# Last weight parts loaded into two gating tiles, a weight split ordered behind a copy, and four squares spread out, in a hybrid decoder layer on one core

## The chip, the cores and the metric

The kernel runs on one core of one Trainium2 chip. The metric is the time on the device of one execution, in microseconds (us). Five engines matter here: TensorE (PE in the profile) multiplies matrices, VectorE (DVE) and ScalarE (ACT) do elementwise work, GpSimd (POOL) and SyncE (SP) mostly issue DMA transfers. Each engine takes its own instructions strictly in order. An instruction that has to wait holds up everything behind it on that engine, and a DMA issue that has to wait holds up all later DMA issues of the same engine.

## The reference, cut to what matters

The reference is one decoder layer for 512 tokens of width 1024 in float32: a gated feed-forward block (22 blocks of 128 hidden columns on each side), a mixer of a state-space scan and differential attention, cross-attention into a memory, a second feed-forward block, and a last norm. The change touches the two feed-forward blocks.

```
def rms_norm(x, w):
    y = x32 * lax.rsqrt(jnp.mean(x32 * x32, axis=-1, keepdims=True) + EPS)
    return y.astype(x.dtype) * w

def swiglu(h, w_in, w_out):
    gate, up = jnp.split(h @ w_in, 2, axis=-1)
    return (jax.nn.silu(gate) * up) @ w_out

x = x + 0.5 * swiglu(rms_norm(x, norm_ffn1_w[l]), ffn1_w_in[l], ffn1_w_out[l])
x = x + hybrid_mixer(...)
x = x + memory_cross_attention(...)
x = x + 0.5 * swiglu(rms_norm(x, norm_ffn2_w[l]), ffn2_w_in[l], ffn2_w_out[l])
return rms_norm(x, norm_final_w)
```

## The kernel before, in words

Every operand of a matmul is split into a high and a low half: ScalarE copies it to a rounded high half (`wh` for a weight, `s31h`, `g11h` and so on for activations), VectorE subtracts to get the low half (`wl`, `s31l`, `g11l`), and TensorE adds three products, high by high, high by low and low by high. All of that goes through the helper `split_into` (lines 155 and 156). Raw weights arrive by DMA in tiles named `wr`, of which there are six. There are three tiles each for `wh` and `wl`. A tile name with a fixed number of buffers is reused in turn, and whoever writes it next has to wait until the last reader of its earlier content is done.

The two matrix products of a feed-forward block are done in a scheme of seven products on two-by-two blocks instead of eight, with sums of weight blocks and of activation blocks as operands.

*The input side.* `quad` makes one group of four column blocks. It accumulates in three PSUM banks `qa`, `qe`, `qb` and runs seven products in this order: "11", S1, S2, "12", S3, S4, "22". Each has its own weight, split from a `wr` tile: the first to the seventh split. Between them the banks are copied: `qb<-qa` before S2 adds to `qb` (lines 284 and 289), `u<-qb` before S3 adds to `qb` (line 299), `p<-qe`. `m3` is the sixth weight, and `t4` the seventh.

*The gating.* `ffn_quads` then multiplies the banks by the norm's row, applies silu in a tile `gate`, multiplies by the other half into a tile `th`, and `block_tiles` makes the blocks and sums of `th` (`g11`, `s31`, `s24`, `g`) that are operands of the output side. `gate` and `th` (made by `s4`, four KB a partition) have one buffer each.

*The output side.* The 22 blocks are taken in three runs of 6, 8 and 8, which the code calls thirds. After the groups of a third, `out_blocks` multiplies with the output weights in banks `oa`, `oe`, `ob`, again in seven products, each in two parts of the contraction (`parts`). The first part of a product uses the early groups, and the last part uses the last groups. In the first feed-forward block the weight sums are made here: `fetch` (line 1277) issues the load of a block on SP's queue, and `added` (line 1316) adds a second block to the same tile with an accumulating DMA from POOL's queue, issued after the load has landed. `t1` is such a sum. It is the weight of the product S1 in the bank `oe`, and its raw tile stays in use to the end of `out_blocks`, since `t2` and the last product add to it. `b21` loads the weight of the product "12". In the second feed-forward block all sums are made beforehand in DRAM, and `out_blocks` there only loads.

The two products that come first, "11" in `oa` and S1 in `oe`, alternate by part: `oa` first part, `oe` first part, `oa` last part, `oe` last part. Then come S2, "12", S3, S4 and "22".

*What sets the order.* SP's and POOL's instructions stand in the order in which the code emits them. For TensorE, VectorE and ScalarE a scheduler orders the instructions by its own estimate of when each can run. The code can put an instruction behind others on the scheduler's list with `behind`.

*The last turn.* Before the second feed-forward block the residual is transposed back to tokens by rows: `turn` transposes on TensorE into `pxf` and copies into `x` on ScalarE. With `summed=True` it also squares each copied tile with a row sum (`squared`, line 551, into a tile `junk`). `row_from` turns the row sums into the norm's row, which the first gating of the second block needs.

Of the kernel before, what the change touches and what calls it, by code (L numbers as in the profile page):

```python
# [11 lines left out]
F32 = mybir.dt.float32  # L12
R32 = mybir.dt.float32r
AF = mybir.ActivationFunctionType
# [3 lines left out]
P = 128  # L18
T = 512
# [81 lines left out]
def body(tc, a, dbg=None):  # L101
# [13 lines left out]
    def nm(s):  # L115
        uid[0] += 1
        return f"{s}_{uid[0]}"
# [6 lines left out]
    def s4(s):  # L124
        return sp.tile([P, 4, T // 2], F32, tag=s, name=nm(s), bufs=1)
# [57 lines left out]
    @contextmanager  # L183
    def behind(ins):
        with ExitStack() as after:
            for i in ins:
                after.enter_context(tc.issue_after(i))
            yield

    H = T // 2  # L190
    S1, S2, S3, S4 = "S1", "S2", "S3", "S4"

    def halves(t):
        return t.rearrange("p (f t) -> p f t", f=2)

# [33 lines left out]
    def add_product(ps, w, xs, which, first, ks=None):  # L229

        wh, wl = w
        n = len(xs)
        for f in range(2):
            out = ps[:, f * H : (f + 1) * H]
            for kp in ks or range(n):
                wc = slice((f * n + kp) * P, (f * n + kp + 1) * P)
                xh, xl = xs[kp][which]
                for j, (a_, b_) in enumerate(((wh, xh), (wh, xl), (wl, xh))):
                    od.t += (H + 32) / 2400
                    newest_mm[:] = [nc.tensor.matmul(out, a_[:, wc], b_, start=first and f == 0 and kp == 0 and j == 0, stop=kp == n - 1 and j == 2, skip_group_check=True).ins]  # L240
                yield
# [9 lines left out]
    def split_w(raw):  # L251
        hi = wp.tile([P, D], R32, tag="wh", name=nm("wh"))
        lo = wp.tile([P, D], R32, tag="wl", name=nm("wl"))
        newest[:] = [split_into(hi, lo, raw)[0].ins]
        return hi, lo

    def quad(xs, src, ready, fresh=False):

        b12, b11, b22, b21 = src[0], src[1], src[2], src[3]
        m1 = raw_w(b11)
        if ready:
            t, t2, m2, m7, m3 = raw_w(ready[0]), raw_w(ready[1]), raw_w(b21), raw_w(b12, b22), raw_w(b22)
            t4 = m2
        else:
            t, m3, m2, m7 = raw_w(b12, b11), raw_w(b22), raw_w(b21), raw_w(b12, b22)  # L270
            t2 = t4 = t
        a_ps = acc("qa")
        e_ps = acc("qe")
        b_ps = acc("qb")
        w1, w5 = split_w(m1), split_w(t)
        second = list(newest)
        if fresh:

            n = len(xs)
            yield from add_product(a_ps, w1, xs, "11", True, range(n - 1))  # L280
            yield from add_product(e_ps, w5, xs, S1, True, range(n - 1))
            yield from add_product(a_ps, w1, xs, "11", False, range(n - 1, n))
            with behind(second):
                S.activation(b_ps, a_ps, AF.Copy)  # L284
            yield from add_product(e_ps, w5, xs, S1, False, range(n - 1, n))
        else:
            yield from add_product(a_ps, w1, xs, "11", True)
            with behind(second):
                S.activation(b_ps, a_ps, AF.Copy)
            yield from add_product(e_ps, w5, xs, S1, True)  # L290
        p5 = s2("p5")
        S.activation(p5, e_ps, AF.Copy)
        if not ready:
            V.tensor_tensor(t2, t, m3, ALU.add)
        yield from add_product(b_ps, split_w(t2), xs, S2, False)
        if not ready:
            V.tensor_tensor(t4, t2, m2, ALU.add)
        u2 = s2("u2")
        S.activation(u2, b_ps, AF.Copy)  # L299
        V.tensor_tensor(e_ps, e_ps, u2, ALU.subtract)  # L300
        yield from add_product(a_ps, split_w(m2), xs, "12", False)
        w7 = split_w(m7)
        if ready:
            V.tensor_tensor(t4, t2, m2, ALU.add)
        yield from add_product(b_ps, w7, xs, S3, False)
        c22 = s2("c22")
        V.tensor_tensor(c22, p5, b_ps, ALU.subtract)
        yield from add_product(e_ps, split_w(m3), xs, S4, False)
        yield from add_product(b_ps, split_w(t4), xs, "22", False)
        yield (a_ps, b_ps), (e_ps, c22)  # L310

# [238 lines left out]
    def squared(k, src):  # L550
        S.activation(s2("junk"), src, AF.Square, accum_out=squares[:, k : k + 1])

    def row_from(st, apart, rows=1.2):
        both = small("nboth", 4, bufs=2)
        V.tensor_tensor(both, squares[:, :4], squares[:, 4:], ALU.add)
        yield from st.from_sums(both, apart, rows)
# [81 lines left out]

    def bc_c(t):
        return t[:, None, :].to_broadcast([P, 4, 16])  # L640

    def flat(t):
        return t.rearrange("p a b -> p (a b)")

    def col64(s):
        return cp.tile([P, 4, 16], F32, name=s)
# [622 lines left out]
    def out_blocks(blocks, sums, g, col4, ncol4, each=None, finale=None, clean=True, n=None, by_dma=False):  # L1269
# [2 lines left out]
        n = n or len(g)  # L1272
        parts = [(k, min(k + 2, n)) for k in range(0, n, 2)]

        def fetch(of, part):
            raw = wp.tile([P, (part[1] - part[0]) * T], F32, tag="wr", name=nm("wr"), bufs=6)
            nc.sync.dma_start(raw, of[:, part[0] * T : part[1] * T])
            return raw

# [19 lines left out]
        def product(ps, of, which, first=False, ready=None):  # L1299
            for part in parts:  # L1300
                w = ready if ready and part == parts[0] else weights(of, part)
                for t in range(2):
                    yield from some(ps[t], w, which, part, t, first)
# [6 lines left out]

        t_raw = {}

        def added(of, more):
            def make(part):
                raw = fetch(of, part)
                G.dma_start(raw, more[:, part[0] * T : part[1] * T], accum_op=ALU.add)
                return raw
            return make

        def t1(part):  # L1320
            t_raw[part] = added(blocks[B12], blocks[B11])(part)
            return t_raw[part]

        def t2(part):
# [2 lines left out]
            return t_raw[part]  # L1327

        def b21(part):
            later[part] = fetch(blocks[B21], part)  # L1330
            return later[part]

        def t4(part):
            G.dma_start(t_raw[part], blocks[B21][:, part[0] * T : part[1] * T], accum_op=ALU.add)
# [29 lines left out]
        for t in range(2):  # L1364
            u2.append(s2("u2"))
            S.activation(u2[t], b_ps[t], AF.Copy)
            V.tensor_tensor(e_ps[t], e_ps[t], u2[t], ALU.subtract)
        yield from product(a_ps, b21 if here and not by_dma else blocks[B21], "12")
        for part in later:
            V.tensor_tensor(t_raw[part], t_raw[part], later[part], ALU.add)  # L1370
        later.clear()
# [83 lines left out]
            yield from out_blocks(a[f"f2b{c}"], wsum[c], g, col4, ncol4, *((norm, store) if at_end else (None, None)), clean=c == 0)  # L1455

    def turn_last():
        yield from turn(1, summed=True)
        od.spawn(row_from(st_2, 8.0), 3.0)

    od.add(turn_last())
    od.add(ffn2())
# [89 lines left out]
```

## Time and profile before

| | |
|---|---|
| median of three runs | 1316.02 us (1313.1 to 1317.21) |
| the profiled execution's own time | 1314.69 us |
| its span, first to last instruction | 1312.8 us |
| TensorE busy | 1290.0 us |
| VectorE busy | 969.8 us |
| ScalarE busy | 707.5 us |
| mean granted TensorE clock | 0.998 |

The profile is of one execution. In a row of the timeline the first number is the start in us from the span's beginning, the second the length, then engine, source line, operation, output<-inputs, shape, how many were merged, and, in brackets, how long the engine had been idle before it and what ended that. SPq is SP's queue of DMA issues. A matmul's length covers the whole pipeline, and matmuls overlap, so the pace is the distance from start to start: about 0.12 us for 256 columns and 0.23 us for 512. Busy shares are averages over stages; what an edit is worth is read at its place.

### The profile page before, as it was taken

The page shows a single profiled execution, that of the slowest core. Times are in us where ns is not written, and L with a number is a line of the kernel's source. Part 1 is how long each engine was busy: PE and PEld are TensorE (multiplying, and loading weights), DVE is VectorE, ACT ScalarE, POOL GpSimd, SP SyncE. Part 2 cuts the span into 40 slices and gives each one's busy share as a digit, 9 for nine tenths or more (in the row PEclk, how much of TensorE's full clock was granted, in tenths as well). Part 3 has the DMA queues.
Part 4 walks back from the last instruction along what each step waited for, and adds up shares of the span by engine and source line. Part 5 has one row for each costly group of instructions (what it writes and reads, how often), then busy time and mean ns, then how long its engine had stood idle before and what let it go on. Part 6 is the DMA issues. An engine that isn't in the chain of part 4 may idle for free.

```text
span 1312.8 us, 20085 instructions
## 1 busy us (share of the span) xinstructions
PE 1290.0 (98%) x7710; PEld 1125.3 (86%) x7710; DVE 969.8 (74%) x1539; ACT 707.5 (54%) x1207; POOL 130.9 (10%) x153
## 2 busy tenths in 40 slices
PE   9999999999999999999999999999999999999997
PEld 7889988998887778777788878888889999989995
DVE  5987888788776676557867686745668878876886
ACT  6544554565754465346645465534365646555564
POOL 0201001001110011110103022020001000000000
PEclk9999999999999999999999999999999999999999
DMA  9357778766994434763365648684139876655652
GB/s 338 85 160 194 200 178 221 220 180 178 327 295 152 130 73 111 257 188 106 85 182 176 183 133 240 189 221 133 65 98 272 207 233 178 187 197 178 196 191 95
DMA packets 70415, 237.38 MB, mean 181 GB/s; under 512 B 8288, under 2 KB 9792, under 8 KB 69968
## 3 DMA queue, kind: packets, MB, share of 16 engines
q1 hardware_dynamic: 54208, 183.13, 40.4%
q0 software_dynamic: 13168, 45.67, 19.4%
q10 hardware_dynamic: 2944, 7.30, 1.6%
q8 instruction: 60, 0.98, 0.3%
q14 instruction: 35, 0.29, 0.1%
HBM read 233.92 MB, written 50.91 MB: 217 GB/s over the span
## 4 chain that ended last, share of the span: by engine, by line
PE 58%; issue 10%; DVE 4%; ACT 2%; DMA 1%; POOL 1%; POOLq 0%; ACTq 0%; DVEq 0%
PE pm L146 10%; PE qb L240 8%; PE qe L240 5%; PE qa L240 5%; PE pxbc L146 4%; PE ob L1296 3%; PE pcq L146 3%; PE pz L146 3%; PE oa L1296 2%; PE oe L1296 2%; PE pcv L146 2%; PE pq L146 2%; PE pv L146 1%; DVE wl L156 1%; PE pk L146 1%
## 5 line engine op out<-in xcount | busy, mean ns | idle before, releaser
L155 ACT ACTIVATE wh<-wr 128x1024 fp32r<-128x1024 f32 (+1 forms) x329 | 334.2, 1019 | 357.8 <-issue 71.2
L156 DVE TENSOR_TENSOR wl<-wr,wh 128x1024 fp32r<-128x1024 f32 (+1 forms) x329 | 384.7, 1173 | 145.7 <-ACT wh L155 141.9
L777 ACT ACTIVATE ec<-ec,mn 128x512 f32<-128x512 f32 (+3 forms) x64 | 35.3, 554 | 33.7 <-DVE mn L776 33.7
L146 PE MATMUL pxbc<-hnh,wh 128*128 128x512 f32 x128 | 52.6, 411 | 0.0
L146 PE MATMUL pxbc<-hnh,wl 128*128 128x512 f32 x128 | 50.2, 392 | 0.0
L146 PE MATMUL pxbc<-hnl,wh 128*128 128x512 f32 x128 | 50.2, 392 | 0.0
L240 PE MATMUL qb<-s31h,wh 128*128 128x256 f32 x152 | 43.2, 284 | 3.2 <-ACT u L299 3.2
L240 PE MATMUL qb<-s24h,wh 128*128 128x256 f32 x152 | 43.1, 284 | 1.3 <-ACT qb L284 1.3
L240 PE MATMUL qb<-s24h,wl 128*128 128x256 f32 x152 | 43.1, 284 | 0.5 <-DVE wl L156 0.5
L240 PE MATMUL qa<-h11h,wh 128*128 128x256 f32 x152 | 43.1, 283 | 0.0
L240 PE MATMUL qb<-s31h,wl 128*128 128x256 f32 x152 | 43.0, 283 | 0.0
L240 PE MATMUL qa<-h11h,wl 128*128 128x256 f32 x152 | 43.0, 283 | 0.0
L240 PE MATMUL qa<-hmh,wh 128*128 128x256 f32 x152 | 43.0, 283 | 0.0
L240 PE MATMUL qa<-hml,wh 128*128 128x256 f32 x152 | 43.0, 283 | 0.0
L240 PE MATMUL qe<-s24h,wh 128*128 128x256 f32 x152 | 43.0, 283 | 0.0
L240 PE MATMUL qe<-s24l,wh 128*128 128x256 f32 x152 | 43.0, 283 | 0.0
L240 PE MATMUL qe<-s24h,wl 128*128 128x256 f32 x152 | 43.0, 283 | 0.0
L240 PE MATMUL qb<-hmh,wh 128*128 128x256 f32 x152 | 43.0, 283 | 0.0
L240 PE MATMUL qb<-hml,wh 128*128 128x256 f32 x152 | 43.0, 283 | 0.0
L240 PE MATMUL qb<-hmh,wl 128*128 128x256 f32 x152 | 43.0, 283 | 0.0
L240 PE MATMUL qa<-h11l,wh 128*128 128x256 f32 x152 | 43.0, 283 | 0.0
L240 PE MATMUL qa<-hmh,wl 128*128 128x256 f32 x152 | 43.0, 283 | 0.0
(452 smaller groups left out, 4166.7 us busy)
## 6 DMA issues: line engine op xcount, KB each, us to landing
wr<-in_f2q SPq DMA_DIRECT2D x44, 512.0 KB, 4.3
wr<-in_f1q SPq DMA_DIRECT2D x40, 512.0 KB, 4.6
wr<-in_f1b SPq DMA_DIRECT2D x30, 512.0 KB, 5.4
isum<-in_f2q SPq DMA_DIRECT2D x22, 512.0 KB, 5.6
wr<-isum SPq DMA_DIRECT2D x22, 512.0 KB, 4.3
wsum<-in_f2b SPq DMA_DIRECT2D x20, 512.0 KB, 6.6
wr<-wsum SPq DMA_DIRECT2D x20, 512.0 KB, 4.6
wr<-in_f1q POOLq DMA_DIRECT2D x16, 512.0 KB, 6.5
```

What stands on the lines that cost most here:

```text
L146: newest_mm[:] = [nc.tensor.matmul(out, w, x, start=start, stop=stop).ins]
L155: S.activation(hi, src, AF.Copy),
L156: V.tensor_tensor(lo, src, hi.bitcast(F32), ALU.subtract),
L240: newest_mm[:] = [nc.tensor.matmul(out, a_[:, wc], b_, start=first and f == 0 and kp == 0 and j == 0, stop=kp == n - 1 and j == 2, skip_gr ...
L777: S.activation(ec[:, :n], ec[:, :n], AF.Exp, bias=mn, scale=-1.0, accum_out=sm[c][:, i : i + 1])
L1296: newest_mm[:] = [nc.tensor.matmul(ps, a_[:, ts], b_[:, ws], start=first and k == 0 and j == 0, stop=k == n - 1 and j == 2, skip_group_che ...
```

## The change

There are three edits.

1. In `out_blocks` of the first feed-forward block, the last part of `t1` is loaded into the tile `gate` and the last part of `b21` into the tile `th`, instead of two `wr` tiles. The loads keep their place in SP's order. `b21` is now also used by the third third.
2. In `quad`, the split of the sixth weight (`m3`) is ordered behind the copy `u<-qb`.
3. The four squares of the last turn are no longer emitted with the copies but by a new chain, one every 2.0 of the order's own time units, each behind the newest weight split. The norm's row is made after them.

```
@@ quad
-        S.activation(u2, b_ps, AF.Copy)
+        copy = S.activation(u2, b_ps, AF.Copy)
...
-        yield from add_product(e_ps, split_w(m3), xs, S4, False)
+        with behind([copy.ins]):
+            w3 = split_w(m3)
+        yield from add_product(e_ps, w3, xs, S4, False)
@@ out_blocks
-        def fetch(of, part):
-            raw = wp.tile([P, (part[1] - part[0]) * T], F32, tag="wr", name=nm("wr"), bufs=6)
+        def fetch(of, part, spare=None):
+            n = (part[1] - part[0]) * T
+            if spare and part == parts[-1]:
+                raw = flat(s4(spare))[:, :n]
+            else:
+                raw = wp.tile([P, n], F32, tag="wr", name=nm("wr"), bufs=6)
             nc.sync.dma_start(raw, of[:, part[0] * T : part[1] * T])
...
-        def added(of, more):
+        def added(of, more, spare=None):
             def make(part):
-                raw = fetch(of, part)
+                raw = fetch(of, part, spare)
                 G.dma_start(raw, more[:, part[0] * T : part[1] * T], accum_op=ALU.add)
...
-            t_raw[part] = added(blocks[B12], blocks[B11])(part)
+            t_raw[part] = added(blocks[B12], blocks[B11], "gate")(part)
...
         def b21(part):
-            later[part] = fetch(blocks[B21], part)
-            return later[part]
+            raw = fetch(blocks[B21], part, "th")
+            if not by_dma:
+                later[part] = raw
+            return raw
...
-        yield from product(a_ps, b21 if here and not by_dma else blocks[B21], "12")
+        yield from product(a_ps, b21 if here else blocks[B21], "12")
@@ turn_last
-        yield from turn(1, summed=True)
-        od.spawn(row_from(st_2, 8.0), 3.0)
+        yield from turn(1)
+        od.spawn(row_of_last(), 4.0)
+
+    def row_of_last():
+        for k in range(4, KT):
+            with behind(list(newest)):
+                squared(k, x[k])
+            yield 2.0
+        yield from row_from(st_2, 3.0)
```

What this moves is shown at three places. The first is SP's queue at the output side of the second third. The rows in turn load, before: the last part of "11", the last part of `t1` (`wr_2158`), two parts of B22, two parts of B21 (`wr_2225`, `wr_2243`) and the first part of S3's weight. In brackets stand the semaphores that a row waits for.

```order
L1277 DMA wr_2140<-in_f1b 128x1024 [waits DMAHW2_49,DMAHW6_49,DVE_49,Activation_49]
L1277 DMA wr_2158<-in_f1b 128x1024 [waits DMASW3_49,DVE_49]
L1277 DMA wr_2181<-in_f1b 128x1024 [waits DMAHW1_49,DMAHW0_49,DVE_49]
L1277 DMA wr_2200<-in_f1b 128x1024 [waits DVE_49]
L1277 DMA wr_2225<-in_f1b 128x1024 [waits DMAHW4_49,DVE_49]
L1277 DMA wr_2243<-in_f1b 128x1024 [waits DMAHW3_49,DMAHW0_49,DVE_49]
L1277 DMA wr_2265<-in_f1b 128x1024 [waits DMAHW6_49,DVE_49]
```

The same rows with the change:

```order
L1283 DMA wr_2140<-in_f1b 128x1024 [waits DMAHW2_49,DMAHW6_49,DVE_49,Activation_49]
L1283 DMA gate_2158<-in_f1b 128x1024 [waits DVE_49,Activation_49]
L1283 DMA wr_2181<-in_f1b 128x1024 [waits DMAHW0_49,DMASW3_49]
L1283 DMA wr_2200<-in_f1b 128x1024 [waits DMAHW1_49]
L1283 DMA wr_2225<-in_f1b 128x1024
L1283 DMA th_2243<-in_f1b 128x1024 [waits DMAHW3_49,DVE_49]
L1283 DMA wr_2265<-in_f1b 128x1024 [waits DMAHW4_49]
```

The load into `gate` now waits for VectorE and ScalarE, the last users of that tile: the last multiplication `th<-c,gate` and the silu of the third's last group. The load into `th` waits for VectorE, whose last use of the tile is `gl<-th,gh`. The loads between and behind them no longer wait for VectorE to free a `wr` tile.

On TensorE, at the end of the last part of "11" (`oa`) at the same place, before:

```order
L1296 MATMUL oa_2110<-wl_2143,g11h_2088 128x512
L1296 MATMUL oe_2111<-wh_2161,s31h_1920 128x512
L1296 MATMUL oe_2111<-wh_2161,s31l_1921 128x512
L1296 MATMUL oe_2111<-wl_2162,s31h_1920 128x512
L1296 MATMUL oe_2111<-wh_2161,s31h_2097 128x512
L1296 MATMUL oe_2112<-wh_2161,s31h_1920 128x512
```

With the change:

```order
L1302 MATMUL oa_2110<-wl_2143,g11h_2088 128x512
L1357 MATMUL ob_3416<-ones_r 128x512
L1302 MATMUL oe_2111<-wh_2161,s31h_1920 128x512
L1302 MATMUL oe_2111<-wh_2161,s31l_1921 128x512
L1302 MATMUL oe_2112<-wh_2161,s31h_1920 128x512
L1302 MATMUL oe_2112<-wh_2161,s31l_1921 128x512
L1302 MATMUL ob_2113<-wh_2184,s24h_1461 128x512
L1302 MATMUL ob_2113<-wh_2184,s24l_1462 128x512
L1302 MATMUL oe_2111<-wl_2162,s31h_1920 128x512
```

`wh_2161` is the high half of the weight that is now loaded into `gate`. One clearing matmul moved ahead of its first use, and two matmuls of S2 (`ob_2113`) moved in between its uses.

The second place is ScalarE in the second group of the last third, from the split of the fifth weight (`wh_2770`). `wh_2804` is the sixth weight, `wh_2832` the seventh. Before:

```order
L155 ACTIVATE wh_2770<-wr_2620 128x1024
L292 ACTIVATE p_489_2687<-qe_2624 128x512
L155 ACTIVATE wh_2804<-wr_2616 128x1024
L155 ACTIVATE s31h_2712<-s_492_2707 128x512
L155 ACTIVATE wh_2832<-wr_2613 128x1024
L299 ACTIVATE u_496_2735<-qb_2625 128x512
L155 ACTIVATE s24h_2751<-s_493_2708 128x512
L155 ACTIVATE gh_2786<-th_2605 128x512
```

With the change:

```order
L155 ACTIVATE wh_2770<-wr_2620 128x1024
L295 ACTIVATE p_489_2687<-qe_2624 128x512
L155 ACTIVATE s31h_2712<-s_492_2707 128x512
L302 ACTIVATE u_496_2735<-qb_2625 128x512
L155 ACTIVATE s24h_2751<-s_493_2708 128x512
L155 ACTIVATE wh_2804<-wr_2616 128x1024
L155 ACTIVATE gh_2786<-th_2605 128x512
L155 ACTIVATE wh_2832<-wr_2613 128x1024
```

The copy `u<-qb` moved ahead of both weight splits.

The third place is ScalarE at the start of the second feed-forward block, from the last sum of activations. `junk` is a square, `wh_9944` (with the change `wh_9936`) the fourth weight of the first group, `qb<-qa` the bank's copy that S2 waits for. Before:

```order
L155 ACTIVATE s24h_9795<-s_2040_9786 128x512
L551 ACTIVATE junk_9820,squares_232<-x_119 128x512
L551 ACTIVATE junk_9823,squares_232<-x_121 128x512
L551 ACTIVATE junk_9826,squares_232<-x_123 128x512
L551 ACTIVATE junk_9829,squares_232<-x_125 128x512
L284 ACTIVATE qb_9846<-qa_9844 128x512
L292 ACTIVATE p_2069_9910<-qe_9845 128x512
L155 ACTIVATE wh_9944<-wr_9837 128x1024
```

With the change:

```order
L155 ACTIVATE s24h_9795<-s_2040_9786 128x512
L556 ACTIVATE junk_9883,squares_232<-x_119 128x512
L155 ACTIVATE wh_9936<-wr_9829 128x1024
L287 ACTIVATE qb_9838<-qa_9836 128x512
L295 ACTIVATE p_2063_9898<-qe_9837 128x512
L556 ACTIVATE junk_9910,squares_232<-x_121 128x512
L556 ACTIVATE junk_9931,squares_232<-x_123 128x512
```

Three of the four squares moved behind the copy, and the split of the fourth weight moved ahead of it.

More of the change, by code (lines that the diff above doesn't have):

```diff
@@ L191, in body, with flat @@
     S1, S2, S3, S4 = "S1", "S2", "S3", "S4"
+    def flat(t):
+        return t.rearrange("p a b -> p (a b)")
     def halves(t):
@@ L640, in bc_c @@
         return t[:, None, :].to_broadcast([P, 4, 16])
-    def flat(t):
-        return t.rearrange("p a b -> p (a b)")
     def col64(s):
```

## The prediction

> **What bounds the kernel now.** I read the page first, then the list of waits of TensorE, then the timeline at the places that the change touches.
>
> ```profile
> span 1312.8 us, 20085 instructions
> PE 1290.0 (98%) x7710; PEld 1125.3 (86%) x7710; DVE 969.8 (74%) x1539; ACT 707.5 (54%) x1207; POOL 130.9 (10%) x153
> PE qb L240 <- ACT u L299: 3.2, 2, 1.6
> PE qb L240 <- ACT qb L284: 1.3, 1, 1.3
> PE oa L1296 <- DVE g11l L156: 0.8, 1, 0.8
> PE oe L1296 <- DVE s31l L156: 0.7, 1, 0.7
> PE qb L240 <- DVE wl L156: 0.5, 1, 0.5
> ...
> PE pt L150 <- DVE on L846: 0.2, 1, 0.2
> ```
>
> TensorE is busy for 98% of the span, and the list of its waits has only fifteen rows, the longest 3.2 us in total. So an edit can win little: what it removes is a row of this list. It can lose much more, since any new wait of TensorE goes straight into the time. The five rows shown at the top are those that the change can reach: 3.2 for the sixth weight's edit, 1.3 for the squares, and 2.0 in or just behind the output sides.
>
> **Edit 1, the loads in the gating's tiles: second third.** The weight of S1's last part is a sum of two blocks: a load from SP's queue, then an accumulating load from POOL's queue, then the split on ScalarE. Before, these stood at
>
> ```profile
> 173.75 0.33 SPq L1277 DMA_DIRECT2D wr<-in_f1b  x1
> 179.58 0.87 POOL L1316 DMA_DIRECT2D wr<-in_f1b  x1 [8.51 <-DVE wl L156]
> 187.97 0.68 DVE L450 TENSOR_TENSOR th<-c,gate 128x512 f32<-128x512 f32 x1
> 189.83 1.06 ACT L155 ACTIVATE wh<-wr 128x1024 fp32r<-128x1024 f32 x1 [2.51 <-DMA wr<-in_f1b]
> 194.49 0.39 PE L1296 MATMUL oe<-wh,s31h 128*128 128x512 f32 x1
> 198.18 0.39 PE L1296 MATMUL ob<-wh,s24h 128*128 128x512 f32 x1
> ```
>
> The load was issued at 173.75, the accumulation at 179.58, its landing let ScalarE go at 189.83, and TensorE took the result at 194.49. With the change the load goes into `gate`, and the order shows that it waits for the last reader of that tile, the multiplication that ends at 187.97 + 0.68 = 188.65. That is 14.9 us later than the issue before. Nothing on TensorE can cover this: behind the last part of `oa` the order has S1's last part, with two matmuls of S2 among the first six. And everything behind it on SP's queue waits too.
>
> For the two DMAs I have their landing times over the program (the loads of line 1277, then the accumulations of line 1316):
>
> ```profile
> DMA to landing us min/median/max: 2.6/4.6/11.6
> DMA to landing us min/median/max: 4.3/5.9/10.1
> ```
>
> From the load's issue to POOL's issue I take 4.5 us: near the median, since SP's queue will be empty, bounded by the least landing, 2.6, and by the 179.58 - 173.75 = 5.8 at this place before. For the accumulation I take 6.3, a little over the median, because three held-up loads start with it; its bounds are 4.3 and the 189.83 - 179.58 = 10.2 seen here. With 1.1 for the split TensorE can start at 188.65 + 4.5 + 6.3 + 1.1 = 200.6 (196.7 to 205.8). Twelve matmuls of 512 columns at 0.227 us make 2.7, so the part ends at 203.3, where before it ended at 198.18: a loss of 5.1 us (1.2 to 10.3). This already counts the two waits of 0.8 and 0.7 on `g11l` and `s31l`, which fall into it and vanish. The load into `th` waits for the end of that group's splits, some 5 us on. Its weight is taken a whole product later, and S3's sums, queued behind it, two products later, so the same delay of TensorE covers both; I cost them at nothing here.
>
> **Last third.** The same place there:
>
> ```profile
> 310.71 2.35 DVE L156 TENSOR_TENSOR wl<-wr,wh 128x1024 fp32r<-128x1024 f32 x2
> 313.58 0.68 DVE L450 TENSOR_TENSOR th<-c,gate 128x512 f32<-128x512 f32 x1
> 318.09 0.39 PE L1296 MATMUL oe<-wh,s31h 128*128 128x512 f32 x1
> 322.02 0.39 PE L1296 MATMUL ob<-wh,s24h 128*128 128x512 f32 x1
> ```
>
> In the new order one of the two splits at 310.71 stands behind the multiplication, so `gate` is free about 1.2 us earlier than 314.26, at 313.1. The same three terms give 313.1 + 11.9 = 325.0 (321.1 to 330.2), and with the 2.7 of the twelve matmuls the part ends at 327.7 against 322.02: a loss of 5.7 us (1.8 to 10.9).
>
> **First third.** No group with `gate` comes before it, so that load is free. The load into `th` is not:
>
> ```profile
> 72.85 0.33 SPq L1277 DMA_DIRECT2D wr<-in_f1b  x1
> 76.10 0.33 SPq L1277 DMA_DIRECT2D wr<-in_f1b  x1
> 79.92 0.68 DVE L156 TENSOR_TENSOR gl<-th,gh 128x512 fp32r<-128x512 f32 x1
> 80.10 0.90 POOL L1316 DMA_DIRECT2D wr<-in_f1b  x1 [17.38 <-DVE wr L1326]
> 87.11 1.06 ACT L155 ACTIVATE wh<-wr 128x1024 fp32r<-128x1024 f32 x1
> 91.47 0.39 PE L1296 MATMUL ob<-wl,s31h 128*128 128x512 f32 x1
> ```
>
> It moves from 72.85 to the end of `gl<-th,gh`, 80.6. Behind it on SP is the load of S3's first part, at 76.10 before and about 81.0 now. With 4.0 to POOL's issue, 6.3 for the accumulation, and 1.1 and 1.2 for the high and the low half, the low half is there at 93.6, and S3's third matmul took it at 91.47: a loss of 2.1 us (none to 3.4).
>
> **The clock.** TensorE would idle for about 7 us in the second third (oa's last part ends near 193.5) and some 6 in the last. The end of the program shows what such a pause does, and its start what it costs (columns of the windows: the stretch, busy time of PE, PEld, DVE, ACT, POOL, then the granted clock):
>
> ```profile
> 1303.60:1308.10 4.50, 0.00 (x0) 0.00 (x0) 2.50 (x6) 2.18 (x5) 1.22 (x2) 1.00 0.71 265
> 1308.20:1312.80 4.60, 0.00 (x0) 0.00 (x0) 0.00 (x0) 0.00 (x0) 0.00 (x0) 0.50 0.26 98
> 6.86 0.63 PE L146 MATMUL pa<-hml,wah 128*128 128x512 f32 x1
> 7.29 0.65 PE L146 MATMUL pa<-hmh,wal 128*128 128x512 f32 x1
> ```
>
> 4.5 us after the last matmul the granted clock falls to 0.50. At the start a matmul of 512 columns takes 0.43 us instead of 0.23. I take eleven matmuls at the slow pace behind each pause, 11 x 0.2 = 2.2 us each, 4.4 in all; the bounds are nothing and twice that. The Trainium skill (TensorE: Matmul & The Clock Gate, What's actually happening) says that the array drops to half its clock after at least one idle window of about 3.4 us and needs about 3.4 us of sustained work to come back. The end of this trace agrees that it drops, after 4.5 us. By the page's window the slow stretch would cost half of 3.4 us, 1.7 a pause and 3.4 in all, an estimate from that page; the sum would be 1.0 less.
>
> **Edit 2, the sixth weight.**
>
> ```profile
> 257.41 1.06 ACT L155 ACTIVATE wh<-wr 128x1024 fp32r<-128x1024 f32 x1 [1.31 <-PE qa L240]
> 258.38 0.58 ACT L299 ACTIVATE u<-qb 128x512 f32<-128x512 f32 x1
> 259.01 0.39 PE L240 MATMUL qb<-s31h,wh 128*128 128x256 f32 x1 [1.58 <-ACT u L299]
> 301.16 0.39 PE L240 MATMUL qb<-s31h,wh 128*128 128x256 f32 x1 [1.58 <-ACT u L299]
> ```
>
> In two of the nineteen groups the seventh weight's split, which has to wait for the product "12" to give up its tile, stood ahead of the copy `u<-qb`, and S3 waited 1.58 us. In the new order the copy stands ahead of both splits in every group. The gain is 3.2 us. The sixth weight is late next: its low half now stands on VectorE behind a gating multiplication and the subtraction from `qe`, and I take 0.2 off: 3.0 (2.5 to 3.2). In the other seventeen groups the copy was in time, and nothing is won.
>
> **Edit 3, the squares.**
>
> ```profile
> 979.67 0.28 PE L240 MATMUL qe<-s31h,wh 128*128 128x256 f32 x1
> 980.63 0.61 ACT L551 ACTIVATE junk<-x 128x512 f32<-128x512 f32 x1
> 981.24 0.57 ACT L284 ACTIVATE qb<-qa 128x512 f32<-128x512 f32 x1
> 981.87 0.38 PE L240 MATMUL qb<-s24h,wh 128*128 128x256 f32 x1 [1.32 <-ACT qb L284]
> ```
>
> Three squares leave from ahead of the copy, but a weight split of 1.06 us takes their place, and it needs the tile that `qa`'s last product gives up at about 979.7. So the copy starts near 980.8 instead of 981.24: a gain of 0.5 us (0 to 1.3), not the whole wait. The row is made later, and the first gating waits for the end of the group anyway; nothing is lost there.
>
> **The sum.** Also the freed tiles let the first group after the first third load earlier; of its 0.5 us wait I take 0.3. Losses 5.1 + 5.7 + 2.1 + 4.4 = 17.3, gains 3.0 + 0.5 + 0.3 = 3.8, together +13.5 us. The profiled execution took 1314.69 us, so 1328.2. The median shown is 1.3 above that execution, well inside the spread of 4 between the three runs, so I leave the forecast at 1328.2. About 0.3%, 4 us, is what a measurement of this kernel can tell from no change.
>
> **The rivals.** *The clock holds.* A few matmuls fall into the pauses (the table's two small ones in the last third), and the pauses are near the limit seen at the end. Then the 4.4 goes: 1323.8. Against it stands that both pauses are longer than 4.5. *The two DMAs are quick.* With SP's queue empty both could take their least, 2.6 and 4.3. Then the losses are 1.2, 1.8 and 0, the pauses are too short for the clock, and with the gains the sum is -0.8: 1313.9, no change. It decides where the accumulation lands less than 8 us after the multiplication. At this very place it took 10.2 by itself before, so I give it little. *The load is not held up*, that is, the wait for `gate` is for an earlier group's use and the load still starts near 173.75. Then edit 1 costs nothing, takes away the 1.5 us on `g11l` and `s31l`, and the result is 1314.7 - 3.8 - 1.5 = 1309.4, faster. The order's row speaks against it, as it names VectorE and ScalarE and no earlier DMA. *Both accumulations are slow*, 10.2 each as seen here: 5.2 more in the second and 5.2 more in the last third, 1338.6.
>
> **Chances.** 1328 (half), clock holds 0.25, slow accumulations 0.12, quick DMAs 0.08, load not held up 0.05. The first three are slower by over 0.3%, the fourth is within it, the last is faster: 0.05, 0.08, 0.87. The range goes from 1317, between quick and middling DMAs, to 1338.
>
> **What would show it.** Right: on TensorE one wait of 5 to 9 us on the split or the DMA of `gate` in each of the second and the last third, one of 1 to 3 us at S3 in the first, granted clock under 1.00 behind the long ones, no row for `u` at S3, and a wait of about 0.8 for `qb<-qa`. It would be wrong if the load into `gate` is issued before the last group's multiplication, or if TensorE finds S2's matmuls to do meanwhile.

## The result and the profile after

The changed kernel took 1336.61 us (median of 5 runs, 1335.52 to 1338.96), the kernel before 1313.42 on the same chip (1312.38 to 1317.21). The ratio is 1.0173, with a 95% interval of 1.0159 to 1.0186: 1.7% slower. The forecast was 1328.2, with a range from 1317 to 1338.

The page and the list of TensorE's waits of the changed kernel, the rows that answer to those shown of before:

```profile
span 1334.8 us, 20083 instructions
PE 1294.1 (97%) x7710; PEld 1128.9 (85%) x7710; DVE 971.3 (73%) x1539; ACT 707.1 (53%) x1207; POOL 126.2 (9%) x153
```

```profile
PE oe L1302 <- ACT wh L155: 19.5, 2, 10.5
PE ob L1302 <- ACT wh L155: 4.3, 2, 3.6
...
PE qb L243 <- ACT qb L287: 0.8, 1, 0.8
```

Two new rows carry the loss: TensorE waits 10.5 and 9.0 us for the split of S1's last part (`oe`), and 3.6 us at S3 in the first third (`ob`). The row for `u` (3.2) is gone, `qb<-qa` went from 1.3 to 0.8.

The timeline at the second third, where the load into `gate` stands:

```profile
191.94 0.68 DVE L455 TENSOR_TENSOR th<-c,gate 128x512 f32<-128x512 f32 x1
...
192.70 0.33 SPq L1283 DMA_DIRECT2D gate<-in_f1b  x1
...
197.58 0.87 POOL L1322 DMA_DIRECT2D gate<-in_f1b  x1 [24.73 <-DMA gate<-in_f1b]
...
206.97 1.06 ACT L155 ACTIVATE wh<-gate 128x1024 fp32r<-128x1024 f32 x1 [8.98 <-DMA gate<-in_f1b]
...
208.08 0.79 PE L1302 MATMUL oe<-wh,s31h 128*128 128x512 f32 x1 [10.47 <-ACT wh L155]
```

The multiplication frees `gate` at 192.62, and the load starts 0.1 us later: it was held up by exactly that. From there it takes 5.0 us to POOL's issue, 9.4 to the split's start and 1.1 to TensorE: 15.5 in all. In the last third the same chain takes 15.0, of which the accumulation 8.9:

```profile
323.45 0.68 DVE L455 TENSOR_TENSOR th<-c,gate 128x512 f32<-128x512 f32 x1
...
324.20 0.33 SPq L1283 DMA_DIRECT2D gate<-in_f1b  x1
...
329.17 0.86 POOL L1322 DMA_DIRECT2D gate<-in_f1b  x1 [20.27 <-ACT gh L155]
...
338.06 1.06 ACT L155 ACTIVATE wh<-gate 128x1024 fp32r<-128x1024 f32 x1 [7.26 <-DMA gate<-in_f1b]
...
339.17 0.79 PE L1302 MATMUL oe<-wh,s31h 128*128 128x512 f32 x1 [9.04 <-ACT wh L155]
```

In the first third it is the load into `th` that is late, and behind it on SP the loads of S3's sums. The accumulation of S3's first part, issued at 83.43, lets the split go at 91.87, 8.4 us later, and S3 starts behind a wait of 3.6:

```profile
78.82 0.33 SPq L1283 DMA_DIRECT2D th<-in_f1b  x1
...
83.43 1.90 POOL L1322 DMA_DIRECT2D wr<-in_f1b  x2 [32.38 <-DMA wr<-in_f1b]
...
91.87 1.06 ACT L155 ACTIVATE wh<-wr 128x1024 fp32r<-128x1024 f32 x1 [5.95 <-DMA wr<-in_f1b]
...
92.98 0.79 PE L1302 MATMUL ob<-wh,s31h 128*128 128x512 f32 x1 [3.61 <-ACT wh L155]
...
100.01 0.39 PE L1302 MATMUL oe<-wh,s24h 128*128 128x512 f32 x1
```

How the DMA engines and the clock went in the second third, in stretches of 4 us (the last three columns are the granted clock, the DMA engines' busy share, which can come out a little above 1, and GB/s), after and then before:

```profile
186.00:190.00 4.00, 4.00 (x32) 3.83 (x31) 1.92 (x2) 1.95 (x2) 0.00 (x0) 1.00 0.01 4
190.00:194.00 4.00, 4.00 (x19) 3.34 (x18) 3.76 (x6) 1.94 (x4) 0.00 (x0) 1.00 0.06 16
194.00:198.00 4.00, 3.61 (x16) 2.63 (x15) 2.35 (x5) 2.55 (x5) 0.42 (x1) 1.00 0.91 248
198.00:202.00 4.00, 0.00 (x0) 0.00 (x0) 1.23 (x1) 0.00 (x0) 0.44 (x1) 0.87 1.01 396
202.00:206.00 4.00, 0.00 (x0) 0.00 (x0) 0.00 (x0) 0.00 (x0) 0.00 (x0) 0.50 1.05 286
```

```profile
186.00:190.00 4.00, 4.00 (x19) 3.32 (x18) 2.65 (x4) 1.23 (x2) 0.00 (x0) 1.00 0.92 321
190.00:194.00 4.00, 3.11 (x13) 2.05 (x12) 3.07 (x4) 3.02 (x5) 0.66 (x1) 1.00 0.23 89
```

With the change the DMA engines stand idle (share 0.01 and 0.06) while SP waits for `gate`, and are full (0.91 to 1.05) as soon as it is free: every load behind that one goes out at once, and the accumulation into `gate` has to share with them.

Where the 22 us lie is read from the starts of the same matmuls, the first of each output side and the first of the groups behind it. Before, and then after:

```profile
74.68 0.40 PE L1296 MATMUL oa<-wh,g11h 128*128 128x512 f32 x1
...
103.26 0.28 PE L240 MATMUL qa<-h11h,wh 128*128 128x256 f32 x1
...
184.85 0.40 PE L1296 MATMUL oa<-wh,g11h 128*128 128x512 f32 x1
...
225.38 0.28 PE L240 MATMUL qa<-h11h,wh 128*128 128x256 f32 x1
...
309.90 0.40 PE L1296 MATMUL oa<-wh,g11h 128*128 128x512 f32 x1
...
344.63 0.39 PE L1296 MATMUL ob<-wh,gh 128*128 128x512 f32 x1
```

```profile
72.87 0.40 PE L1302 MATMUL oa<-wh,g11h 128*128 128x512 f32 x1
...
108.17 0.28 PE L243 MATMUL qa<-h11h,wh 128*128 128x256 f32 x1
...
189.03 0.40 PE L1302 MATMUL oa<-wh,g11h 128*128 128x512 f32 x1
...
239.57 0.28 PE L243 MATMUL qa<-h11h,wh 128*128 128x256 f32 x1
...
320.83 0.40 PE L1302 MATMUL oa<-wh,g11h 128*128 128x512 f32 x1
...
367.54 0.39 PE L1302 MATMUL ob<-wh,gh 128*128 128x512 f32 x1
```

| stretch | before | after | difference | forecast |
|---|---|---|---|---|
| start to the first output side | 74.7 | 72.9 | -1.8 | 0 |
| first output side | 28.6 | 35.3 | +6.7 | +2.1 |
| groups to the second | 81.6 | 80.9 | -0.7 | -0.3 |
| second output side | 40.5 | 50.5 | +10.0 | +7.3 |
| groups to the last (edit 2) | 84.5 | 81.3 | -3.3 | -3.0 |
| last output side, to its last product | 34.7 | 46.7 | +12.0 | +7.9 |
| the rest (edit 3) | 968.2 | 967.3 | -0.9 | -0.5 |
| sum | 1312.8 | 1334.8 | +22.0 | +13.5 |

(The clock's 4.4 of the forecast stands half with the second, half with the last output side.) The -1.8 at the start is not the change's: kernels that are alike up to there start the first output side at 72.9 or at 74.6 (the changed kernel at 72.87, the one with its two long pauses filled, below, at 74.58).

### The profile page after: what moved, and what is told of

Same layout as the page of the kernel before. It is cut to its first block, busy times and chain, and to the rows that moved or that the text cites. A ratio compares the mean times of both kernels' runs of the same rounds, so it can differ in the third digit from the quotient of the medians.

```text
span 1334.8 us, 20083 instructions
## 1 busy us (share of the span) xinstructions
PE 1294.1 (97%) x7710; PEld 1128.9 (85%) x7710; DVE 971.3 (73%) x1539; ACT 707.1 (53%) x1207; POOL 126.2 (9%) x153
## 4 chain that ended last, share of the span: by engine, by line
PE 77%; issue 13%; DVE 3%; DMA 3%; ACT 2%; POOL 1%; POOLq 0%; SPq 0%; ACTq 0%; DVEq 0%
PE qb L243 12%; PE pm L146 10%; PE qa L243 8%; PE qe L243 8%; PE ob L1302 5%; PE pxbc L146 4%; PE oe L1302 4%; PE pcq L146 3%; PE oa L1302 3%; PE pz L146 3%; DMA gate<-in_f1b 2%; PE pcv L146 2%; PE pg L146 2%; PE pu L146 2%; PE pa L146 2%
## 5 line engine op out<-in xcount | busy, mean ns | idle before, releaser
L155 ACT ACTIVATE wh<-wr 128x1024 fp32r<-128x1024 f32 (+1 forms) x317 | 323.2, 1022 | 332.4 <-issue 58.8
L156 DVE TENSOR_TENSOR wl<-wr,wh 128x1024 fp32r<-128x1024 f32 (+1 forms) x317 | 372.3, 1178 | 140.0 <-ACT wh L155 138.4
L779 ACT ACTIVATE ec<-ec,mn 128x512 f32<-128x512 f32 (+3 forms) x64 | 35.3, 554 | 33.7 <-DVE mn L778 33.7
L243 PE MATMUL qb<-s31l,wh 128*128 128x256 f32 x152 | 43.1, 284 | 0.0
L243 PE MATMUL qe<-s31h,wl 128*128 128x256 f32 x152 | 43.1, 283 | 0.0
```

Of the source, the lines that this page charges most:

```text
L155: S.activation(hi, src, AF.Copy),
L156: V.tensor_tensor(lo, src, hi.bitcast(F32), ALU.subtract),
L779: S.activation(ec[:, :n], ec[:, :n], AF.Exp, bias=mn, scale=-1.0, accum_out=sm[c][:, i : i + 1])
```

## The experiments

Times are compared with runs of the kernel before on the same chip, by the ratio; a run's difference to another run is the difference of their ratios times 1314. Rows and waits of a run are from one profiled execution of it.

**Edits 2 and 3 alone.** Edit 1 is taken back:

```diff
-            t_raw[part] = added(blocks[B12], blocks[B11], "gate")(part)
+            t_raw[part] = added(blocks[B12], blocks[B11])(part)
...
-            raw = fetch(blocks[B21], part, "th")
-            if not by_dma:
-                later[part] = raw
-            return raw
+            later[part] = fetch(blocks[B21], part)
+            return later[part]
...
-        yield from product(a_ps, b21 if here else blocks[B21], "12")
+        yield from product(a_ps, b21 if here and not by_dma else blocks[B21], "12")
```

> Edit 1 is undone, the sixth weight's order and the spaced squares stay. By the prediction's own terms (3.0 for the sixth weight, 0.5 for the squares) 3.5 us under the kernel before: 1310. If these two edits carry part of the loss that the forecast missed, the time is above that of the kernel before by up to 8. If what they remove comes back as another wait, there is no difference. In the list of waits the row for u (3.2) should be gone and the one for qb behind the copy of qa should read 0.8.

Measured: 1319.46 us, ratio 1.0037 (1.0026 to 1.0049). Slower than before, though the wait on `u` was gone and that on `qb<-qa` down to 0.8, and though at the start of the last output side TensorE was 5.1 us ahead of the kernel before (304.85 against 309.90), 1.7 of them from the start of the program. On that output side it lost 9.0 us, to its last product (43.75 against 34.73), and 8.1 of them at one place, S3, with a wait of 5.1 and 3.0 us of slow matmuls behind it. Rows of the timeline there, of VectorE, SP, POOL and TensorE:

```profile
317.39 0.74 DVE L1313 SCALAR_TENSOR_TENSOR x<-oe,col,x 128x512 f32<-128x512 f32 x1
...
318.45 1.22 DVE L1332 TENSOR_TENSOR wr<-wr,wr 128x1024 f32<-128x1024 f32 x1
...
319.69 0.33 SPq L1283 DMA_DIRECT2D wr<-in_f1b  x1
...
327.66 0.87 POOL L1322 DMA_DIRECT2D wr<-in_f1b  x1 [8.16 <-DMA wr<-in_f1b]
...
337.43 0.80 PE L1302 MATMUL ob<-wh,s31h 128*128 128x512 f32 x1 [5.07 <-ACT wh L155]
```

The order of VectorE shows what else changed there (`wr_3462` takes S2's second sum, `x_123` and `x_125` are the updates that wait for TensorE to finish `oe`). Before, and with edits 2 and 3:

```
L156 TENSOR_TENSOR s31l_3400<-s_598_3394,s31h_3399 128x512
L1326 TENSOR_TENSOR wr_3462<-wr_3462,wr_3519 128x1024
L156 TENSOR_TENSOR s24l_3404<-s_599_3395,s24h_3403 128x512
L1307 SCALAR_TENSOR_TENSOR x_123<-oe_3413,col_69_295,x_123 128x512
```

```
L1313 SCALAR_TENSOR_TENSOR x_125<-oe_3414,col_69_295,x_125 128x512
L160 SCALAR_TENSOR_TENSOR hm_3511<-mem_542_3046,par,hm_3511 128x256
L1332 TENSOR_TENSOR wr_3462<-wr_3462,wr_3519 128x1024
```

The second sum now stands behind both updates. This is put down to edit 2, which moved the sixth weight's split; edit 3's place lies 650 us later, but the two edits were not run apart. The sum gives up a `wr` tile at 319.67, SP's load of S3's last part starts at 319.69, its accumulation at 327.66, and TensorE waits 5.1 us.

**Only the load into `gate`.**

```diff
-            raw = fetch(blocks[B21], part, "th")
-            if not by_dma:
-                later[part] = raw
-            return raw
+            later[part] = fetch(blocks[B21], part)
+            return later[part]
```

> The loads into th go back to wr, the loads into gate stay (and edits 2 and 3). Theory one, that the two output sides lose their time each by itself: the first third's loss goes (4.2 us by the start of the same matmuls in the two traces), the waits of 10.5 and 9.0 us in the second and the last third stay: 1336.6 - 4.2 = 1332. Theory two, that it is the load into th, issued a microsecond before the accumulation into gate, that makes that accumulation take 9 us instead of 6: each of the two waits falls by some 2 to 3 us, too: 1327.

Measured: 1332.44 us, 1.0136 (1.0122 to 1.0151), as theory one had it. The two waits are as long as with `th`:

```profile
PE oe L1302 <- ACT wh L155: 20.1, 2, 10.8
```

So the load into `th` is not what makes the accumulation slow; in its place another load of the same size goes out at the same time.

**Only the load into `th`.**

```diff
-            t_raw[part] = added(blocks[B12], blocks[B11], "gate")(part)
+            t_raw[part] = added(blocks[B12], blocks[B11])(part)
```

> The loads into gate go back to wr, the loads into th stay (and edits 2 and 3). If th costs nothing in the second and the last third, as forecast, only the first third's 4.2 us remain on top of 1310: 1314. If S3's sums behind it on SP's queue are late in those thirds too, they show a wait of 2 to 5 us each at S3 and the time is 1318 to 1324.

Measured: 1329.5 us, 1.0117 (1.0100 to 1.0134), above both expectations.

```profile
PE ob L1302 <- ACT wh L155: 10.7, 4, 5.3
```

S3's sums, behind the load into `th` on SP's queue, are late in all three thirds: waits of 1.0, 5.3 and 3.3 us at S3, with slow matmuls behind the last two, and one of 1.1 at S2 in the last third. Over edits 2 and 3 alone, `gate` costs 13.0 us, `th` 10.5, both together 17.9: where `gate` holds TensorE up by 9 or 10 us, S3's sums come in time, and their wait is hidden.

**Edit 1 alone.**

```diff
-        with behind([copy.ins]):
-            w3 = split_w(m3)
-        yield from add_product(e_ps, w3, xs, S4, False)
+        yield from add_product(e_ps, split_w(m3), xs, S4, False)
...
-        yield from turn(1)
-        od.spawn(row_of_last(), 4.0)
+        yield from turn(1, summed=True)
+        od.spawn(row_from(st_2, 8.0), 3.0)
```

> Edit 1 alone: the sixth weight and the squares stand as in the kernel before. If edits 2 and 3 give in the changed kernel what the forecast gave them, 3.5 us, this is 1340 and the row for u (3.2) is back. If they cost there what they cost by themselves (5.7), it is 1331. The waits on S1's last part should be those of the changed kernel, 10.5 and 9.0, within 1.

Measured: 1341.34 us, 1.0202 (1.0181 to 1.0223). The row for `u` is back with 3.2, the waits on S1's last part are 10.3 and 10.1. Within edit 1's company, edits 2 and 3 give 3.8 us (1.0202 less 1.0173; with both intervals 0.5 to 7). The forecast's 3.5 fits, and so would other values. By themselves they cost 4.9. S3's late sum is hidden behind the longer wait for `gate`, as that of `th` is.

**Fewer loads beside the accumulation.** In the first kernel the plain load into `gate` goes out from POOL's queue, in the second S2's two loads go ahead of it on SP's; both have only the load into `gate`.

```diff
-            nc.sync.dma_start(raw, of[:, part[0] * T : part[1] * T])
+            (G if spare and part == parts[-1] else nc.sync).dma_start(raw, of[:, part[0] * T : part[1] * T])
```

```diff
+        ahead = {}
+
         def t1(part):
+            if n > 3 and part == parts[-1]:
+                ahead.update((p, fetch(blocks[B22], p)) for p in parts)
...
-            more = fetch(blocks[B22], part)
+            more = ahead.pop(part) if part in ahead else fetch(blocks[B22], part)
```

> Only the load into gate stays (as in the run of that alone, 1332.4), but it is issued from POOL's queue, in which the accumulation stands right behind it; SP's queue no longer waits for gate, and the loads behind it go out as in the kernel before. Theory one, that the accumulation takes 9.3 us because the loads that were held up on SP's queue run beside it: it falls to 5 to 6.5, each of the two waits by 3 to 4, and the time to 1325. Theory two, that an accumulation of this size takes this long there in any case (10.2 in the kernel before): waits and time stay, 1332, or rise a little with the slower issue of POOL.

> Only the load into gate stays, on SP's queue, but the two loads for S2's sums are issued ahead of it in the second and the last third. Theory one: with two of the four to six loads beside it gone, the accumulation falls from 9.3 to 7 or less, and the time from 1332.4 to 1327. Theory two: the accumulation stays at 9, the time at 1332.

With POOL's queue: 1328.29 us, 1.0103 (1.0082 to 1.0123). With S2's loads ahead: 1330.43 us, 1.0119 (1.0094 to 1.0144). The second third of the first one:

```profile
189.62 0.56 POOL L1283 DMA_DIRECT2D gate<-in_f1b  x1 [20.64 <-DVE g11l L156]
194.30 0.86 POOL L1322 DMA_DIRECT2D gate<-in_f1b  x1 [4.12 <-DMA gate<-in_f1b]
```

```profile
199.88 1.06 ACT L155 ACTIVATE wh<-gate 128x1024 fp32r<-128x1024 f32 x1 [5.64 <-DMA gate<-in_f1b]
```

| kernel | accumulation to the split's start, second and last third | TensorE's two waits |
|---|---|---|
| changed kernel | 9.4, 8.9 | 10.5, 9.0 |
| only `gate` | 9.4, 9.2 | 10.8, 9.3 |
| S2's loads ahead | 8.0, 8.4 | 9.5, 8.4 |
| `gate` from POOL's queue | 5.6, 7.6 | 7.1, 7.6 |

In these traces, the less goes out beside it, the shorter the accumulation and the wait. That bears out theory one in its direction. By the time alone it is clear for POOL's queue (4.3 us under only `gate`, 1 to 7.6 by the intervals) and not for S2's loads ahead (2.2, within the intervals). The sizes expected were too large for both kernels (1325 and 1327): in the last third the POOL queue's accumulation still had company (DMA share 0.67 and 0.84 from 320 to 328), and 7 us of each wait stay even there, since the load starts only when `gate` is free and two transfers follow each other.

**The clock.** Matmuls that clear a bank fill TensorE's pauses, in one kernel the two long ones, in the other the first third's.

```diff
+                if which == S1 and here and n > 3 and part == parts[-1]:
+                    with behind(list(newest_mm)):
+                        for _ in range(40):
+                            nc.tensor.matmul(b_ps[1], ones_r, ones_r[:, None, :].to_broadcast([P, 4, P]), start=True, stop=True)
```

> The changed kernel, with forty matmuls of 512 columns (9.1 us at full pace) that clear ob put in front of S1's last part in the second and the last third, so that TensorE works through the two long pauses; they compute nothing that is kept but the clearing. If the slow matmuls behind the pauses (1.5 and 2.6 us over the normal pace) are the clock's doing, the time falls by 4.1 to 1332.5, and the granted clock stays at 1.00 there. If they are slow for another reason (operands that come late), it stays at 1336.6. If the fillers themselves stand in the way, it rises.

Measured: 1336.62 us, 1.0165 (1.0148 to 1.0183): no gain that can be told from none. In the second third the clock stayed at 1.00 (1.00 from 196 to 212), but the product that had been slow was hardly shorter, 9.4 us instead of 9.7 from S1's last part to the product "12": TensorE, now at full pace, waited 1.2 us for the high half of the weight and 0.5 for the low half. In the last third the clock fell all the same, behind the filled stretch:

```profile
340.00:344.00 4.00, 3.48 (x11) 1.85 (x10) 3.87 (x5) 1.31 (x3) 2.59 (x3) 0.70 0.79 182
344.00:348.00 4.00, 4.00 (x10) 2.34 (x9) 2.92 (x4) 3.44 (x6) 1.40 (x2) 0.50 0.97 158
```

```diff
+                if which == S3 and here and n == 3 and part == parts[0]:
+                    fill = acc("fill")
+                    with behind(list(newest_mm)):
+                        for _ in range(16):
+                            nc.tensor.matmul(fill, ones_r, ones_r[:, None, :].to_broadcast([P, 4, P]), start=True, stop=True)
```

> The changed kernel with sixteen matmuls of 512 columns on ones, into a bank that nothing reads, between the product of the first third before S3 and S3: 3.6 us at full pace, as long as TensorE's pause of 3.6 there. Nothing else moves on any engine. If the twelve slow matmuls behind the pause (2.9 us over their normal pace) are the clock's doing, the granted clock stays at 1.00 there, S3 takes 4.6 (4.1 and the 0.5 that the low half is late) instead of 7.0, and the time is 1336.6 - 2.4 = 1334. If they are slow because their operands come late, S3 still takes 7.0, and the time stays or rises.

```profile
92.93 0.39 PE L1302 MATMUL ob<-wh,s31h 128*128 128x512 f32 x1
...
97.60 0.39 PE L1302 MATMUL oe<-wh,s24h 128*128 128x512 f32 x1
```

S3 takes 4.7 us instead of 7.0, as expected of the clock, and S4 starts 2.4 us earlier than in the changed kernel. But the time is 1337.65 us, 1.0182 (1.0162 to 1.0202): nothing of it is left at the end. Of the 2.4 us 1.2 were left at S1's last part in the second third, which starts when its accumulation lands, and 0.1 at S2 behind it, where the slow stretch after the pause was longer than in the changed kernel. So the slow clock behind a pause is shown, by this run, to be what makes the matmuls slow; that it adds its length to the time is not.

**The second sum ahead of the updates.** Three kernels with edits 2 and 3. The first writes S2's sums ahead of the two updates of x in all thirds of ffn1, the second only in the last third and behind the first sum's split, the third is the second with the load into `gate` in the first third alone.

```diff
+        w2 = None
+        if by_dma:
+            w2, second = weights(t2, parts[0]), t2(parts[1])
+            sums[2] = lambda part: second
         for t in range(2):
             update(t + 2, 1, e_ps[t], 1, False)
-        yield from product(b_ps, sums[2], S2)
+        yield from product(b_ps, sums[2], S2, ready=w2)
...
-            t_raw[part] = added(blocks[B12], blocks[B11])(part)
+            t_raw[part] = added(blocks[B12], blocks[B11], "gate" if n == 3 else None)(part)
```

(The last two lines are those of the third kernel. The first has the two sums ahead as `{part: t2(part) for part in parts}`, without the split between them.)

> Edits 2 and 3 without edit 1, as in the run before that was slower than forecast, and in the output sides of ffn1 S2's two sums are written ahead of the two updates of x from oe, so that VectorE adds S2's second part before it waits for oe. Theory: in that earlier run the second sum stood behind both updates, so that the buffer that it gives up, and with it the load of S3's last part, came 4 us late, and TensorE waited 5.1 us at S3 in the last third and ran slow behind it for 2.9. Then that wait goes to under 1 and the time is that of the kernel before less 5: 1309. If the load of S3 is late because it shares the DMA engines (7 us instead of 5.4), a wait of 3 or more stays there, and the time is 1314 or more.

> Edits 2 and 3 without edit 1, and only in the last third S2's second sum is written ahead of the two updates of x, behind the split of the first; the second third stays as in the run of edits 2 and 3, where its two waits on g11l and s31l (0.8 and 0.7) had shrunk to one of 0.5. By adding up: the kernel before, less 3.2 for u, 0.5 for qb, 1.0 in the second third, and less than 1 of new wait in the last: 4 to 5 us under the kernel before, 0.3 to 0.4%. If the gain in the second third comes from the run's DMA times and not from the order, it is no better than the run with the sums first in all thirds (0.16% under the kernel before).

> The same, and the load of S1's last part goes into gate in the first third alone, where no gating stands ahead of it. Theory: gate is free there, so the load is issued without a wait, nothing is lost, and a wr buffer is free earlier for the loads behind it: same time as without it or up to 0.5 us less. If even there the load waits or holds up SP's queue, a wait of 1 us or more appears on S1's or S2's last part in the first third.

Measured: 1312.35 us, 0.9984 (0.9970 to 0.9997); 1312.36 us, 0.9983 (0.9973 to 0.9994); 1311.92 us, 0.9976 (0.9964 to 0.9987). The wait at S3 went from 5.1 to 0.4 in the first and to 0.6 in the second, each with 0.5 more on the low half:

```profile
PE ob L1302 <- ACT wh L155: 0.6, 1, 0.6
```

That the place of one VectorE sum cost edits 2 and 3 their gain is shown: with it moved they are 7 us faster (1.0037 against 0.9984 and 0.9983). The sizes expected, 4 to 5.5 us under the kernel before, were too large: 2.1, 2.2 and 3.2. In the first kernel waits on `g11h`, `g11l` and `s31l` of 0.8, 0.8 and 0.7 were there in the second third, and one of 1.4 on the low half of S2's first part in the last; in the second one, waits of 1.5 and 0.8 stand in the first group after the first third. The third is the fastest kernel of the study, faster than both kernels compared; that its load into `gate` adds anything to the second cannot be told from these intervals.

## Why the prediction was right or wrong

- **The sign and the mechanism: right.** The load into `gate` starts at the end of the gating's last multiplication in both thirds (0.1 us behind it), TensorE has nothing else to do, and the row for the split of `gate` is the largest of its waits. The rival that the load is not held up falls with the row at 192.70, the one of quick DMAs with accumulations of 9.4 and 8.9, and the one that the clock holds with the 0.50 from 202 on. Two of the forecast's own signs came out larger than it said: 10.5 for a wait of 5 to 9, and 3.6 at S3 for one of 1 to 3. The time lies inside the range, 1.4 below its end, and that is in part luck, since the profiled run was 1.8 faster before the first output side for no reason of the change.
- **The accumulation, 6.3 us: too small, and the step that failed.** It took 9.4, 8.9 and, in the first third, 8.4: 3.1, 2.6 and 2.1 more, 7.8 in all. The other two terms held: 5.0 instead of 4.5 to POOL's issue, 1.1 for the split. The forecast took a little over the median of the program, with the remark that three held-up loads start at the same time; the two runs with fewer loads beside it show that the number depends on this company (5.6 where the least ran beside it, and there the chain from the release of `gate` to TensorE took 200.98 - 189.05 = 11.9, the forecast's own sum). The 10.2 that the forecast read at this very place was the nearer row: it too had company (DMA share 0.74, 0.87 and 0.92 from 178 to 190 before). The rival that used it, 1338.6, came nearest to the time.
- **First third, 2.1 us: 6.7.** Besides the accumulation it has a term that the forecast left out, the clock behind a pause of 3.6 us, 7.0 - 4.1 = 2.9 us of slow matmuls in S3 (18 matmuls at 0.227 make 4.1).
- **The clock, 4.4 us for two pauses.** The clock did fall to 0.50 behind all three. What the matmuls behind a pause lost can be counted at the pace of 0.227: 2.9 at S3 in the first third, 1.6 in the second (14 matmuls from 208.08 to 212.83, 4.75 instead of 3.18) and 2.5 in the last (the 12 of S1's last part from 339.17 to 344.39, 5.22 instead of 2.72). The 1.6 and 2.5 make 4.1 against the forecast's 4.4, so its 2.2 a pause is right in size. As a price it is not confirmed: filling the pauses took the slow matmuls away at two places and left the time as it was. By the Trainium skill (TensorE: Matmul & The Clock Gate, What's actually happening) the array's clock is halved after an idle window of about 3.4 us; the traces agree for the changed kernel's pauses of 3.6 and more, and differ for one of 2.9 (below).
- **`th` in the second and the last third, nothing: right only beside `gate`.** By itself it costs waits of 5.3 and 3.3 there.
- **Edit 2, -3.0, and edit 3, -0.5: right in the changed kernel** (-3.3 in the groups of the last third, -0.9 in the rest, 3.8 by the two ratios with their wide interval), and wrong as prices of their own: without edit 1's pauses the same edits cost 4.9, by an order that changed in a place where nothing was written anew. The forecast looked at what stands beside the copy, not at what the planner does elsewhere.

In sum: 8.5 us were missing between spans. The accumulations account for 7.8, the first third's clock for 2.9; against that the start of the profiled run was 1.8 faster. The remainder, under 1, is not assigned.

## What to carry to other kernels

A tile that stands idle most of the time is only free when its last reader is done, and a load into it from an in-order queue holds up every load behind it; price the first transfer after the release with all of them beside it, from a row with such company, not by the median. Where a planner orders an engine, compare the whole order of that engine after an edit, not just the place edited: one sum behind two updates cost here more than the edit won. Costs of late transfers at neighbouring places do not add up, since the longest hides the others, so an edit's price alone and its price in company can differ in sign.

## What the runs showed of the hardware

The granted clock stayed at 1.00 behind a pause of 2.7 us of edit 1 alone, and fell behind those of 2.9 us and more (the second row is of the kernel with the long pauses filled):

```profile
93.82 0.50 PE L1300 MATMUL ob<-wh,s31h 128*128 128x512 f32 x1 [2.66 <-ACT wh L155]
```

```profile
93.97 0.50 PE L1302 MATMUL ob<-wh,s31h 128*128 128x512 f32 x1 [2.90 <-ACT wh L155]
```

Both pauses had a second wait of 0.5 us behind them, 1.3 us later, on the low half. After the 2.9 us the clock fell only 2 us after matmuls had begun again at 93.97, to 0.50 from 96 to 98. Nor is the delay fixed: in the changed kernel the clock fell 2.3 us into the first third's pause (the last matmul ends at 89.37, the clock is 0.85 from 91 to 92 and 0.50 after) and 3.3 into the second third's (197.6; 0.97 from 200 to 201), and at the end of the kernel before it held for 4.5. And in the last third of the kernel with the long pauses filled it fell to 0.50 though TensorE had waited for no more than 1.1 and 0.5 us behind the filled stretch, while two such waits in its second third (1.2 and 0.5) left the clock at 1.00. What tells the two apart was not tried. In the changed kernel, behind a pause of 3.6 us the slow matmuls lost no less than behind one of 9 or 10: 2.9 us in the one case, 1.6 and 2.5 in the others.

From its issue to the start of the split that waits for it, an accumulation of 512 KB took 5.6 us where the DMA engines were busy for 0.37 of the 4 us in which it started and 0.93 of the next four (`gate` from POOL's queue, 192 to 200), and 9.4 where they were busy throughout (1.03 and 1.02 in the same stretch with only `gate`).
